# Two or four plain feed-forward blocks ahead of the paired ones

## The chip, the cores and the metric

The kernel runs on one core of a Trainium2 chip. The metric is the device time of one execution in microseconds; a kernel is run several times and the median is given. A single execution is also profiled, and the profile's span and rows belong to that execution alone.

The engines of the core that matter here are TensorE (PE in the profile; its weight loads are PEld), VectorE (DVE), ScalarE (ACT), GpSimd (POOL), which issues some transfers, and SyncE (SP), which issues most of the others. Each engine runs its own list of instructions in order and waits on semaphores for the others.

## The reference

One layer of a hybrid decoder, for 512 prompt positions and 64 sample positions (576 columns in all), with a model width of 1024:

```python
h = rms_norm(x, g_mix)
z = h @ w_in                      # pooling input, q, f, i, gate, ga, gb
ya = pool_branch(z) @ w_pool_up
yb = hgrn2_branch(z) @ w_hgrn_up
merged = sigmoid(ga) * ya + sigmoid(gb) * yb
x = x + merged @ w_out

h2 = rms_norm(x, g_ffn)
x = x + (silu(h2 @ w_ffn_gate) * (h2 @ w_ffn_up)) @ w_ffn_down

h3 = rms_norm(x, g_ple)
x = x + sigmoid(h3 @ w_ple_gate) * (p @ w_ple_proj)
y = rms_norm(x, g_final)
```

The feed-forward width is 2816, that is 22 blocks of 128 columns. All is float32.

## The kernel before

**Layout.** Activations lie transposed: a tile has 128 rows (features) and T = 576 columns (positions), so the width of 1024 is eight tiles. The columns are cut in two halves of HT = 288 (H0, H1). Every product is made with operands split in two: a high part in the rounded matmul format (fp32r) and a low part, which is what is missing; a product is high x high, high x low and low x high, three matmuls.

**A plain unit** (`mm`, L141 on) multiplies one 128-column block of weights by all eight tiles: 8 x 2 halves x 3 = 48 matmuls of 288 columns. A feed-forward block is a gate unit and an up unit, 96 matmuls. The weights of a plain unit need no work on VectorE: ScalarE makes the high part and the negated raw weights, and a transfer from POOL that adds (L88) completes the low part.

**A pair** (`pair`, L969) handles two neighbouring blocks at once by a Strassen-Winograd scheme: seven products in place of eight, each of 12 matmuls, 84 in all. Its products are named after the operand on the activation side: B11, S1, S2, B21, U3, and, done one pair later, U4 and B22. The order on TensorE is written out: `in_order` (with `state["pe"]`) hangs each group of matmuls behind the one before it. For a pair VectorE makes sums of the weights (`p_s1` L841 on, `p_s2` L846 on) and the low parts of two weight operands (`p_lo`, L855: B and C); ScalarE makes the high parts (L853), and two transfers from POOL complete the low parts of A and D.

**The forms.** The activation side of a pair, too, is made of sums: `form(k)` (L807) makes, from the residual tiles k and k+4, the normed values (two instructions at L811), four differences and sums of half width (L814 to L818), and splits them into the tiles fa, fb, fs and fu, each with a high part by ScalarE (L804) and a low part by VectorE (L805). There are four forms, k = 0 to 3, and every product of a pair runs over all four. They need `rn`, the reciprocal root of the mean square. The temporary tiles of a form are the same two rotating buffers (`ctile`, tags chi and clo) that later hold weight operand C.

**The order of the feed-forward stage.** NPL = 4 blocks, 0 to 3, go as plain units on residual tiles that carry the gain but not yet `rn`; `rn` is applied when a result leaves PSUM (L1122 and L1125), so these blocks can start before `rn` is known. It becomes known inside block 0. The forms are made beside the plain blocks: form 0 in block 0, forms 1 and 2 in block 1, form 3 in block 2, none in block 3. Beside the last plain block the first pair's weights are prepared (`p_all`, a generator stepped three times by `next(first)`). Then come the pairs: gate and up for blocks 4 and 5, 6 and 7, and so on to 20 and 21, with the down projections between them as soon as six activated blocks are there. The activated products of a gate and an up pair are turned into forms for the down projection by `ac_form`, for blocks 0 and 1 in the first pair and for 2 and 3 in the second.

Instructions of one engine are ordered by a scheduler that goes by program order and takes a later instruction when an earlier one is not ready in its own reckoning; so evictions and forms interleave on VectorE.

The same `pair` and `form` serve the gates of the mixer earlier, with four units of another projection beside the four forms.

Of the kernel before, what the change touches and what calls it, by code (L numbers as in the profile page):

```python
# [18 lines left out]
HT = 288  # L19
TA = 320  # L20
KD = 8
NPL = 4
EPS = 1e-6
WINDOWS = (2, 4, 8, 16)
UW = 15 + TP + 8 * 23
# [3 lines left out]
def trunk(ctx: ExitStack, tc: tile.TileContext, a, o):  # L29
# [43 lines left out]
    def hi_lo(pl=wp, tag="", bufs=3):  # L73
        return [pl.tile([P, 1024], F32R, name="w" + n, tag="w" + n + tag, bufs=bufs) for n in ("hi", "lo")]
# [34 lines left out]
    plain0 = len(seq)  # L109
    for m in range(NPL):  # L110
        seq += [a["w_ffn_gate"][m], a["w_ffn_up"][m]]
# [5 lines left out]
    def ahead(n_raw, n_split):  # L117
        while state["raw"] < min(n_raw, state["lim"]):
            i = state["raw"]
            raws[i] = raw_load(seq[i], seq[i].shape[-1])  # L120
            state["raw"] += 1
        while state["split"] < min(n_split, state["lim"]):
            i = state["split"]

            kw = dict(pl=es_pool["fp"], tag="z", bufs=2) if i >= len(seq) - 2 else {}
            if plain0 <= i < dn0 or i in (dn0 + 1, dn0 + 2) or up0 + 4 <= i < out0 and i % 2:
                kw["src"] = seq[i]
            splits[i] = split(raws.pop(i), seq[i].shape[-1], **kw)
            state["split"] += 1
# [643 lines left out]
    pairs = [(kind, m, 0) for m in range(0, KD, 2) for kind in ("ga", "gb")]  # L773
    for j in range(NPL, 22, 2):
        pairs.append(("gate", j, 0))
# [12 lines left out]
    def bank(t):  # L788
        return ps1.tile([P, 512], F32, name="b" + t, tag=t)[:, 0:HT]
# [3 lines left out]
    def two_banks():  # L793
        banks.reverse()
        return [bank(t) for t in banks[0]]

    def ctile(t, n=1024, dt=F32R):
        return fp.tile([P, 1024], dt, name="c" + t, tag="c" + t, bufs=2)[:, 0:n]
# [27 lines left out]
    def p_load(n):  # L826
        q = pr[n]
        q["ra"] = raw_load(q["src"][0], 2 * q["W"])
        q["rb"] = rb = fp.tile([P, 1024], F32, name="rb", tag="rb", bufs=2)
        nc.sync.dma_start(out=rb[:, 0:2 * q["W"]], in_=q["src"][1])  # L830

    def p_a(n):
        q = pr[n]
        q["A"] = u = hi_lo()
        split_dma(q["ra"], u, q["src"][0])

    def p_d(q):
        q["D"] = [fp.tile([P, 512], F32R, name="d" + x, tag="d" + x, bufs=2) for x in "hl"]
        split_dma(q["rb"][:, q["K"][1]], q["D"], q["src"][1][:, q["K"][1]])

    def p_s1(q):  # L841
        ra, rb, (K0, K1) = q["ra"], q["rb"], q["K"]
        tt(out=rb[:, K1], in0=rb[:, K0], in1=rb[:, K1], op=ADD)  # L843
        tt(out=rb[:, K0], in0=rb[:, K0], in1=ra[:, K0], op=SUB)

    def p_s2(q):  # L846
        ra, rb, (K0, K1) = q["ra"], q["rb"], q["K"]
        tt(out=ra[:, K0], in0=ra[:, K0], in1=rb[:, K1], op=SUB)  # L848
        tt(out=ra[:, K1], in0=ra[:, K1], in1=ra[:, K0], op=ADD)  # L849

    def p_hi(q, n, tiles, raw):
        q[n] = tiles
        nc.scalar.copy(out=tiles[0][:, 0:2 * q["W"]], in_=q[raw][:, 0:2 * q["W"]])  # L853

    def p_lo(q, n, raw):  # L855
        hi, lo = (t[:, 0:2 * q["W"]] for t in q[n])
        tt(out=lo, in0=q[raw][:, 0:2 * q["W"]], in1=hi.bitcast(F32), op=SUB)  # L857

    def p_b(q):
        p_hi(q, "B", hi_lo(), "rb")  # L860
        p_lo(q, "B", "rb")

    def prod(out, q, u, second, name, seeded):

        hi, lo = q[u]
        kw = {"skip_group_check": True} if seeded else {}
        n = q["W"] // P
        with in_order():
            for k in range(n):
                wh, wl = (w[:, second * q["W"] + k * P:second * q["W"] + (k + 1) * P] for w in (hi, lo))  # L870
                xh, xl = q["f"][name][k]
                nc.tensor.matmul(out=out, lhsT=wh, rhs=xh, start=k == 0 and not seeded, stop=False, **kw)  # L872
                nc.tensor.matmul(out=out, lhsT=wh, rhs=xl, start=False, stop=False, **kw)  # L873
                i = nc.tensor.matmul(out=out, lhsT=wl, rhs=xh, start=False, stop=k == n - 1, **kw)  # L874
        state["pe"] = i.ins

    def c22(q):
        q["cz"] = fp.tile([P, T], F32, name="cz", tag="cz", bufs=1)
        tt(out=q["cz"][:, H1], in0=q["b"], in1=q["p5"], op=ADD)  # L879

    def c21(q):
        tt(out=q["cz"][:, H0], in0=q["c"], in1=q["p5"], op=ADD)  # L882

    def p5_copy(q):
        q["p5"] = fp.tile([P, HT], F32, name="p5", tag="p5", bufs=1)
        nc.scalar.copy(out=q["p5"], in_=q["d"])
# [34 lines left out]
    def ac_split(j):  # L921
        t = gg.pop(j)
        xh, xl = (pl.tile([P, T], F32R, name="a" + tag, tag=tag) for pl, tag in ahl[2 * (j - 18):2 * (j - 17)])
        ac.append((xh, xl))
        nc.scalar.copy(out=xh, in_=t)
        tt(out=xl, in0=t, in1=xh.bitcast(F32), op=SUB)
# [42 lines left out]
    def pair(n):  # L969

        q, p = pr[n], pr[n - 1] if n > run[0] else None
        nq = pr[n + 1] if n + 1 < run[1] else None
        more = n + 2 < run[1]
        if more:
            p_load(n + 2)
        q.update({t: bank(t) for t in "ab"})
        prod(q["a"], q, "A", 0, "B11", False)
        if p:
            c22(p)
        if "B" not in q:  # L980
            p_b(q)
        seed = act(q["b"], q["a"], AF.Copy)
        if n == 0:
            with tc.issue_after(seed.ins):
                p_hi(nq, "A", hi_lo(), "ra")
            p_lo(nq, "A", "ra")
        q.update({t: bank(t) for t in "cd"})
        if p:
            prod(p["c"], p, "D", 0, "U4", True)
            c21(p)  # L990
            prod(p["b"], p, "C", 1, "B22", True)
        else:
            prod(q["d"], q, "B", 0, "S1", False)
        if nq:
            with tc.issue_after(seed.ins):
                p_d(nq)
            p_s1(nq)
        else:
            state["lim"] = len(seq) if run[0] else dn0
            ahead(state["use"] + 2, state["use"] + 1)  # L1000
        if p:
            evict(n - 1)
        if nq:
            p_s2(nq)
        prod(q["b"], q, "C", 0, "S2", True)
        x = act(q["c"], q["b"], AF.Copy)  # L1006
        with tc.issue_after(x.ins):
            if nq:
                p_hi(nq, "C", [ctile(t) for t in ("hi", "lo")], "ra")
        prod(q["a"], q, "A", 1, "B21", True)  # L1010
        if nq:
            p_lo(nq, "C", "ra")
        if more:
            with tc.issue_after(x.ins):
                p_a(n + 2)
        else:
            ahead(state["use"] + 3, state["use"] + 2)
        if p:
            prod(q["d"], q, "B", 0, "S1", False)
        p5_copy(q)  # L1020
        if n < run[0] + 2:
            if run[0]:
                ac_form(2 * (n - run[0]))
        elif pairs[n - 1][0] == "up" and pairs[n - 1][1] < 18:
            ac_form(pairs[n - 1][1])
        elif pairs[n - 1][0] == "up":
            for j in (18, 19):
                ac_split(j)
        prod(q["b"], q, "B", 1, "U3", True)
# [32 lines left out]
    run = [0, 8]  # L1062
# [11 lines left out]
    for n in range(*run):  # L1074
        pair(n)
# [25 lines left out]
    run[:] = run[1], len(pairs)  # L1101
    for j in range(NPL):
        if j == 0:
            spare = two_banks()
            pg, u = two_banks(), next_unit()
            mm(pg, u, hx, ks=range(0, 7))
            rn = rms(spare, [ctile(t, T) for t in ("hi", "lo")])
            mm(pg, u, hx, ks=range(7, KD))
        else:
            pg = unit_mm(hx, two_banks())  # L1110
        if j == NPL - 1:
            first = p_all(run[0])
            next(first)
            next(first)
        pu = unit_mm(hx, two_banks())
        for k in ((0,), (1, 2), (3,), ())[j]:
            form(k, g_ffn, rn, forms)
        if j == NPL - 1:
            next(first)
        g0, tg = tmpa(), tmpb()  # L1120
        for sl, z in zip((H0, H1), pg):
            tt(out=g0[:, sl], in0=z, in1=rn[:, sl], op=MULT)  # L1122
        act(g0, g0, AF.Silu)
        for sl, z in zip((H0, H1), pu):
            tt(out=tg[:, sl], in0=z, in1=rn[:, sl], op=MULT)  # L1125
        gg[j] = pers.tile([P, T], F32, name="stash", tag=("hh3", "hl7", "ssum")[j]) if j < NPL - 1 else g0
        tt(out=gg[j], in0=g0, in1=tg, op=MULT)
# [244 lines left out]
```

## Time and profile before

| what | us |
|---|---|
| median of 3 runs | 836.67 |
| lowest, highest | 836.52, 840.22 |
| the profiled execution's own time | 838.23 |
| its span in the profile | 836.2 |
| block 0 and its rms, from the first matmul to block 1 | 378.88 to 392.22 |
| block 1 | 392.22 to 404.94 |
| blocks 2 and 3 | 404.94 to 430.49 |
| first pair's first matmul | 430.49 |

The span is what the profile shows of the execution; the execution's own time is a little longer. Rows of a timeline give the start from the beginning of the span, the duration, the engine, the line of the kernel, the operation and its output and inputs; in square brackets stands the idle time of the engine ahead of it and what ended it. Tiles in PSUM are named ba, bb, bc and bd. Instructions of one engine overlap a little, so the distance from start to start is what one costs when the engine is full.

### The profile page before, as it was taken

What the parts mean: (1) busy time and instruction counts of PE and PEld (TensorE: products, weight loads), DVE (VectorE), ACT (ScalarE), POOL (GpSimd) and SP (SyncE); (2) the same over time, 40 slices, a digit from 0 to 9 for tenths busy, and PEclk for the clock granted to TensorE, in tenths of its full rate; (3) what the DMA queues carried; (4) which work ended last, traced back from release to release, by engine and by line L of the source; (5) the groups of instructions that cost most, each with busy time, mean ns of one, the idle gap of its engine ahead of it and who ended that gap; (6) DMA issues with size and microseconds to landing.
All of it is one profiled execution on the core that took longest, in us unless ns stands there. A gap on an engine that the chain in (4) does not pass through costs nothing.

```text
span 836.2 us, 15184 instructions
## 1 busy us (share of the span) xinstructions
PE 822.1 (98%) x6092; PEld 807.7 (97%) x6092; DVE 605.6 (72%) x1005; ACT 504.5 (60%) x826; POOL 114.1 (14%) x194
## 2 busy tenths in 40 slices
PE   8999999999999999999999999999999999999996
PEld 6999899999999999999999999999999999998996
DVE  7877776764787776547988688777787777558846
ACT  7356435666777665446667667766676666645534
POOL 6304110000111110000111121112211121000000
PEclk9999999999999999999999999999999999999998
DMA  7521220322747674246866787657777678453103
GB/s 233 164 84 51 76 105 29 126 105 80 181 107 183 165 172 140 76 108 144 186 130 142 149 208 194 157 123 175 181 173 164 132 158 214 113 156 101 52 1 113
DMA packets 38758, 111.95 MB, mean 134 GB/s; under 512 B 4896, under 2 KB 8992, under 8 KB 38688
## 3 DMA queue, kind: packets, MB, share of 16 engines
q1 hardware_dynamic: 24000, 74.51, 27.1%
q0 software_dynamic: 12528, 33.30, 23.5%
q10 hardware_dynamic: 2160, 3.19, 1.0%
q8 instruction: 47, 0.77, 0.4%
q14 instruction: 23, 0.19, 0.1%
HBM read 105.98 MB, written 5.00 MB: 133 GB/s over the span
## 4 chain that ended last, share of the span: by engine, by line
PE 91%; DVE 3%; DMA 2%; ACT 1%; issue 1%; POOL 1%; SPq 0%; DVEq 0%
PE bb L872 7%; PE bb L873 7%; PE bb L874 7%; PE mm L155 5%; PE mm L153 5%; PE mm L157 5%; PE ba L874 4%; PE ba L873 4%; PE ba L872 4%; PE bd L874 2%; PE bd L873 2%; PE bd L872 2%; PE bc L873 2%; PE bc L874 2%; PE bc L872 2%; PE ba L153 2%
## 5 line engine op out<-in xcount | busy, mean ns | idle before, releaser
L78 ACT CAST whi<-raw 128x1024 fp32r<-128x1024 f32 (+2 forms) x48 | 46.6, 972 | 70.6 <-PE mm L155 32.8
L153 PE MATMUL mm<-hh,whi 128*128 128x288 f32 x320 | 71.2, 304 | 1.1 <-DVE ta L358 0.9
L155 PE MATMUL mm<-hl,whi 128*128 128x288 f32 x320 | 70.8, 301 | 1.3 <-DVE hl L242 1.3
L157 PE MATMUL mm<-hh,wlo 128*128 128x288 f32 x320 | 69.5, 299 | 0.4 <-DVE wlo L79 0.4
L87 ACT ACTIVATE wlo<-raw 128x1024 fp32r<-128x1024 f32 (+1 forms) x49 | 49.2, 1004 | 26.3 <-PE ba L874 18.4
L79 DVE TENSOR_TENSOR wlo<-raw,whi 128x1024 fp32r<-128x1024 f32 (+2 forms) x48 | 56.7, 1184 | 10.4 <-ACT whi L78 9.8
L857 DVE TENSOR_TENSOR clo<-raw,chi 128x1024 fp32r<-128x1024 f32 (+1 forms) x38 | 43.3, 1140 | 27.8 <-ACT chi L853 27.7
L153 PEld LDWEIGHTS mm<-hh,whi 128*128 128x128 f32 x320 | 52.9, 193 | 4.0 <-ACT whi L78 1.6
L155 PEld LDWEIGHTS mm<-hl,whi 128*128 128x128 f32 x320 | 52.3, 191 | 2.5 <-DVE hl L242 1.9
L157 PEld LDWEIGHTS mm<-hh,wlo 128*128 128x128 f32 x320 | 52.3, 191 | 0.7 <-DVE wlo L79 0.6
L857 DVE TENSOR_TENSOR wlo<-rb,whi 128x1024 fp32r<-128x1024 f32 (+1 forms) x38 | 43.3, 1139 | 10.9 <-ACT whi L853 10.7
L853 ACT CAST chi<-raw 128x1024 fp32r<-128x1024 f32 (+1 forms) x38 | 36.9, 971 | 9.8 <-DVE raw L849 9.8
L853 ACT CAST whi<-rb 128x1024 fp32r<-128x1024 f32 (+1 forms) x38 | 37.3, 982 | 6.3 <-PE bb L873 2.8
L87 ACT ACTIVATE dl<-rb 128x512 fp32r<-128x512 f32 (+1 forms) x38 | 22.7, 598 | 30.0 <-PE bc L874 28.2
L1006 ACT ACTIVATE bc<-bb 128x288 f32<-128x288 f32 x38 | 15.0, 395 | 41.6 <-PE bb L874 41.6
L91 ACT CAST whi<-raw 128x1024 fp32r<-128x1024 f32 (+1 forms) x37 | 36.0, 972 | 0.0
L843 DVE TENSOR_TENSOR rb<-rb 128x512 f32<-128x512 f32 (+1 forms) x38 | 24.6, 647 | 8.0 <-ACT dh L91 8.0
L882 DVE TENSOR_TENSOR cz<-bc,p 128x288 f32<-128x288 f32 x38 | 17.3, 456 | 14.6 <-PE bc L874 14.3
L879 DVE TENSOR_TENSOR cz<-bb,p 128x288 f32<-128x288 f32 x38 | 17.3, 456 | 14.2 <-PE bb L874 9.1
L848 DVE TENSOR_TENSOR raw<-raw,rb 128x512 f32<-128x512 f32 (+1 forms) x38 | 24.6, 647 | 1.2 <-ACT whi L91 0.5
L88 POOL DMA_DIRECT2D wlo<-in_w_ffn_gate x13 | 11.1, 855 | 103.8 <-ACT wlo L87 103.8
L849 DVE TENSOR_TENSOR raw<-raw 128x512 f32<-128x512 f32 (+1 forms) x38 | 24.6, 647 | 0.8
(789 smaller groups left out, 3227.6 us busy)
## 6 DMA issues: line engine op xcount, KB each, us to landing
raw<-in_w_in SPq DMA_DIRECT2D x26, 512.0 KB, 3.4
raw<-in_w_ffn_gate SPq DMA_DIRECT2D x13, 512.0 KB, 4.1
raw<-in_w_ffn_up SPq DMA_DIRECT2D x13, 512.0 KB, 5.3
wlo<-in_w_ffn_gate POOLq DMA_DIRECT2D x13, 512.0 KB, 5.5
wlo<-in_w_ffn_up POOLq DMA_DIRECT2D x13, 512.0 KB, 6.3
rb<-in_w_ffn_gate SPq DMA_DIRECT2D x9, 512.0 KB, 4.6
rb<-in_w_ffn_up SPq DMA_DIRECT2D x9, 512.0 KB, 5.3
raw<-in_w_dn SPq DMA_DIRECT2D x12, 384.0 KB, 3.7
```

The costliest lines, as they stand in the source:

```text
L78: nc.scalar.copy(out=hi[:, cs], in_=raw[:, cs])
L79: tt(out=lo[:, cs], in0=raw[:, cs], in1=hi[:, cs].bitcast(F32), op=SUB)
L87: neg = act(lo, raw, AF.Copy, scale=-1.0)
L91: nc.scalar.copy(out=hi, in_=raw)
L153: nc.tensor.matmul(out=out[h], lhsT=wh, rhs=xh[:, h * HT:(h + 1) * HT], start=first, stop=False)
L155: nc.tensor.matmul(out=out[h], lhsT=wh, rhs=xl[:, h * HT:(h + 1) * HT], start=False, stop=False)
L157: i = nc.tensor.matmul(out=out[h], lhsT=wl, rhs=xh[:, h * HT:(h + 1) * HT], start=False, stop=last)
L853: nc.scalar.copy(out=tiles[0][:, 0:2 * q["W"]], in_=q[raw][:, 0:2 * q["W"]])
L857: tt(out=lo, in0=q[raw][:, 0:2 * q["W"]], in1=hi.bitcast(F32), op=SUB)
L872: nc.tensor.matmul(out=out, lhsT=wh, rhs=xh, start=k == 0 and not seeded, stop=False, **kw)
L873: nc.tensor.matmul(out=out, lhsT=wh, rhs=xl, start=False, stop=False, **kw)
L874: i = nc.tensor.matmul(out=out, lhsT=wl, rhs=xh, start=False, stop=k == n - 1, **kw)
```

## The change

The constant goes from 4 to 2. Two places that spelled out the old count go with it: the pairs in which `ac_form` takes plain blocks, and the distribution of the forms, which are now form 0 in block 0 and forms 1, 2 and 3 in block 1. Blocks 2 and 3 become a gate and an up pair, ahead of those for 4 and 5.

```diff
-NPL = 4
+NPL = 2
...
         p5_copy(q)
-        if n < run[0] + 2:
+        if run[0] <= n < run[0] + NPL // 2:
             if run[0]:
                 ac_form(2 * (n - run[0]))
         elif pairs[n - 1][0] == "up" and pairs[n - 1][1] < 18:
...
         pu = unit_mm(hx, two_banks())
-        for k in ((0,), (1, 2), (3,), ())[j]:
+        for k in ((0,), (1, 2, 3))[j]:
             form(k, g_ffn, rn, forms)
         if j == NPL - 1:
             next(first)
```

The list of pairs and the list of plain weights are built from NPL, so the two blocks leave the one and enter the other. `p_all` for the first pair is stepped beside block 1, the last plain one. The branch of `pair` on the mixer's side (run[0] = 0) does nothing in either kernel.

## The prediction

> **What bounds the kernel now.** The first view is the page: the share of each engine and the chain of waits.
>
> ```profile
> span 836.2 us, 15184 instructions
> PE 822.1 (98%) x6092; PEld 807.7 (97%) x6092; DVE 605.6 (72%) x1005; ACT 504.5 (60%) x826; POOL 114.1 (14%) x194
> PE 91%; DVE 3%; DMA 2%; ACT 1%; issue 1%; POOL 1%; SPq 0%; DVEq 0%
> ```
>
> TensorE (PE) is busy 98% of the span and carries 91% of the chain that ended last. So fewer matmuls shorten the kernel, and every wait put on TensorE lengthens it by its whole length. The averages hide that the change sits in one stage, so the second view is busy time by stretch, cut at the feed-forward blocks. The columns are the stretch, its length, the busy time (and instructions) of PE, PEld, DVE, ACT and POOL, the granted TensorE clock, the DMA share and GB/s.
>
> ```profile
> 389.21:415.44 26.23, 26.23 (x199) 26.16 (x199) 26.23 (x54) 19.88 (x29) 4.27 (x5) 1.00 0.78 167
> 404.94:417.76 12.82, 12.82 (x98) 12.75 (x97) 11.18 (x22) 8.23 (x12) 1.70 (x2) 1.00 0.87 188
> 417.76:430.49 12.73, 12.73 (x99) 12.73 (x98) 10.04 (x18) 7.27 (x10) 0.84 (x1) 1.00 0.65 155
> 438.45:449.57 11.12, 11.12 (x86) 11.12 (x85) 9.31 (x14) 9.48 (x17) 2.35 (x3) 1.00 0.60 144
> 449.57:460.70 11.13, 11.13 (x87) 11.13 (x86) 8.70 (x16) 6.77 (x13) 1.90 (x3) 1.00 0.57 126
> ```
>
> The second and third rows are plain blocks 2 and 3 (each a gate and an up unit, 96 matmuls); the last two are whole pairs (84 matmuls). TensorE has no idle time in any of them. The first row is the one to remember: from 389.21 to 415.44 VectorE (DVE) is busy 26.23 of 26.23 us. In this stretch TensorE and VectorE are both full, and only the order of the work keeps VectorE off the path. The third view, VectorE's instructions in order of time, says with what it is full.
>
> ```profile
> 385.53 3.77 DVE L277 RECIPROCAL rn<-rn 128x288 f32<-128x288 f32 x2 [1.03 <-ACT rn L276]
> 389.21 0.40 DVE L1122 TENSOR_TENSOR ta<-ba,rn 128x288 f32<-128x288 f32 x1
> 389.53 0.81 DVE L811 SCALAR_TENSOR_TENSOR chi<-res,C,rn 128x576 f32<-128x576 f32 x1
> ...
> 407.57 0.46 DVE L1122 TENSOR_TENSOR ta<-bb,rn 128x288 f32<-128x288 f32 x1
> 407.94 0.45 DVE L1125 TENSOR_TENSOR tb<-bc,rn 128x288 f32<-128x288 f32 x1
> 408.30 0.45 DVE L1125 TENSOR_TENSOR tb<-bd,rn 128x288 f32<-128x288 f32 x1
> ...
> 409.39 0.76 DVE L1127 TENSOR_TENSOR stash<-ta,tb 128x576 f32<-128x576 f32 x1
> 410.06 0.82 DVE L811 SCALAR_TENSOR_TENSOR clo<-res,C,rn 128x576 f32<-128x576 f32 x1
> ...
> 413.30 0.46 DVE L1122 TENSOR_TENSOR ta<-ba,rn 128x288 f32<-128x288 f32 x1
> 413.67 0.45 DVE L1122 TENSOR_TENSOR ta<-bb,rn 128x288 f32<-128x288 f32 x1
> 414.09 0.76 DVE L805 TENSOR_TENSOR fs3l<-chi,fs3h 128x576 fp32r<-128x576 f32 x1
> 414.77 0.75 DVE L805 TENSOR_TENSOR fu3l<-clo,fu3h 128x576 fp32r<-128x576 f32 x1
> 415.44 0.68 DVE L844 TENSOR_TENSOR rb<-rb,raw 128x512 f32<-128x512 f32 x1
> ```
>
> The reciprocal of the norm ends near 389.3, and nothing of the forms can start before it. The last form tile (fu3l) ends where the next instruction starts, at 415.44. In between stand the four forms, the evictions of blocks 0 and 1, and two instructions of block 2. An eviction is four instructions with 0.37 us from start to start (407.57, 407.94, 408.30) and one with 0.67 (409.39 to 410.06): 2.1 us. Block 2's two take 0.8 (413.30 to 414.09). So four forms take 26.2 - 2 x 2.1 - 0.8 = 21.2 us, **5.3 us each**. In the kernel before, the first pair reads them at 430.49, 15 us after they are done.
>
> ```profile
> 430.49 0.30 PE L872 MATMUL ba<-fa0h,whi 128*128 128x288 f32 x1
> ```
>
> **The change part by part.** *Removed and added on TensorE.* Blocks 2 and 3 go (404.94 to 430.49, 25.55 us) and two pairs come (11.12 + 11.13 = 22.25 us): **-3.3 us**. That is 192 matmuls for 168, at 0.133 us each. The new pairs load no more than the units they replace, and the pair rows above (DVE 9.31 and 8.70 of 11.1 us) leave each some 2 us of VectorE to spare.
>
> *Moved: the forms.* The first pair now starts where block 2 started, at 404.94. Its five products run in a fixed order, B11, S1, S2, B21, U3, each 12 matmuls (1.59 us). Without waits S1 would start at 406.5 and S2 at 408.1. B11 needs the last tile fa3; S1 needs fs3 and the low part of weight B; S2 needs the low part of weight C; the others need fb3 and fu3. All of it is VectorE work that can start at 389.2:
>
> - eviction of block 0, 2.1 us, and four forms, 21.2 us: 412.5;
> - the weight sums of the first pair and two subtractions for the low parts of B and C, priced by these rows (starts are some 0.08 us closer than durations): 3 x 0.6 + 2 x 1.15 = 4.1 us: 416.6;
> - the eviction of block 1, 2.1 us, as far as it comes ahead of these: up to 418.7.
>
> ```profile
> 420.00 0.69 DVE L848 TENSOR_TENSOR raw<-raw,rb 128x512 f32<-128x512 f32 x1 [0.48 <-ACT whi L91]
> 420.73 0.69 DVE L849 TENSOR_TENSOR raw<-raw 128x512 f32<-128x512 f32 x1
> 422.59 1.23 DVE L857 TENSOR_TENSOR clo<-raw,chi 128x1024 fp32r<-128x1024 f32 x1 [1.17 <-ACT chi L853]
> 425.14 1.22 DVE L857 TENSOR_TENSOR wlo<-rb,whi 128x1024 fp32r<-128x1024 f32 x1
> ```
>
> The low part of C cannot be made early: its tiles (chi, clo) are those in which the forms are made. The low part of B can; before, it came after C because its buffer was freed by the last plain block's gate unit (first row below), now it is freed by block 1's, which ends where its up unit starts (second row).
>
> ```profile
> 424.06 1.05 ACT L853 CAST whi<-rb 128x1024 fp32r<-128x1024 f32 x1 [1.50 <-PE bb L155]
> ...
> 398.58 0.29 PE L153 MATMUL bc<-hh,whi 128*128 128x288 f32 x1
> ```
>
> So I take B first: S1 starts near 416.5 and S2 near 417.7, the middle of 416.6 and 418.7. S2's first matmul with a low part stands 0.27 us behind its start, so the wait is 417.7 - 408.4 = 9.3 us; with casts on ScalarE between the links I take **+10 us** (bounds 6.9 and 12.0, worked out below). The matmuls behind the wait are all queued behind it: TensorE runs in order.
>
> *The other queues.* The raw weights of the first pair come where plain block 2's came, into the slot that block 1's gate unit frees; that load was issued at 380.84, and block 2's low part by POOL at 397.64, seven us ahead of 404.94. So no transfer becomes late.
>
> ```profile
> 380.84 0.33 SPq L70 DMA_DIRECT2D raw<-in_w_ffn_gate  x1
> 397.64 0.85 POOL L88 DMA_DIRECT2D wlo<-in_w_ffn_gate  x1 [7.17 <-ACT wlo L87]
> ```
>
> The vector work that is late (block 1's eviction, ac_form(0)) falls behind S2, where the pairs' spare 2 us each take it up; I cost it at nothing, and at up to 2 us if the second pair's sums come behind it.
>
> *The clock.* A wait of this length is something the trace before has only at its end.
>
> ```profile
> 760.00:766.00 6.00, 4.27 (x31) 4.19 (x32) 5.52 (x10) 3.62 (x5) 0.00 (x0) 1.00 0.18 74
> ...
> 828.00:831.00 3.00, 1.04 (x6) 0.72 (x6) 1.90 (x4) 2.53 (x6) 0.00 (x0) 0.81 0.00 0
> 831.00:833.00 2.00, 0.00 (x0) 0.00 (x0) 0.06 (x1) 0.00 (x0) 0.00 (x0) 0.50 0.92 349
> ```
>
> With 1.7 us idle of six the clock stays 1.00; when the matmuls end for good it falls to 0.50 (a mean of 0.81 over three us is 1.1 us at half) within some two us. How long it stays low after work resumes no row shows: nothing at one end, two whole products at half clock (24 matmuls x 0.133 = +3.2 us) at the other. The end row is the nearer one (idle after dense work), so I take one product: **+1.6 us**. The Trainium skill, TensorE: Matmul & The Clock Gate, section on the HAM clock gate, says that an idle window of about 3.4 us halves the clock and that a busy window of the same length restores it. By its figures one such gap would cost an estimated 1.7 us, and the sum would be +8.4 in place of +8.3; the end rows agree with the fall, and no run here shows the return.
>
> **Sum:** -3.3 + 10 + 1.6 = +8.3 us. The span of 836.2 would be 844.5, the profiled execution's own 838.23 us would be 846.5. The median of the runs, 836.67, stands 1.56 below that execution; the difference carries over: **845.0 us**.
>
> **The rivals.** *No loss of clock.* The wait comes in two pieces (B11's last three matmuls run between), and the gate does not close: -3.3 + 10 = +6.7, 843.4 us. For it: the 1.00 beside gaps of 1.7 us; against: each piece is over 3 us.
>
> *The best order.* VectorE leaves block 1's eviction and fu3 (0.67 us) until after the low part of C. S2 then starts at 416.6 - 0.67 - 0.6 (one weight sum done in the idle time ahead of the reciprocal) = 415.3, a wait of 6.9; without loss of clock the sum is +3.6, 840.3 us, within 0.5%.
>
> *Not slower at all.* The pair eats its forms in the order in which they are made, so the wait could vanish: -3.3, 833.4 us. It decides at the price of a form: all that S2 needs must be done by 408.4, so four forms have 408.4 - 389.2 - 2.1 - 4.1 = 13.0 us, 3.2 each. The rows say 5.3 with VectorE already full, so this is nearly excluded.
>
> *Longer.* The low part of C comes ahead of that of B, as before, and with block 1's eviction ahead of both: S1 waits from 406.8 to 418.7, 12.0 us, and the clock costs 3.2: +11.9, 848.6 us. With 2 us lost in the second pair, 850.6.
>
> **How the numbers follow.** Forecast 0.50; no loss of clock 0.20; best order 0.10; not slower 0.03; longer 0.17. A measurement here can tell about 0.5%, 4.2 us, from no change. Slower by more: 0.50 + 0.20 + 0.17 = 0.87; within: 0.10; faster: 0.03 (and -3.3 alone would hardly be told from no change). The range leaves out the 0.03, a part of the best order and the far end of the longest: 840.0 to 850.5.
>
> **What would show it.** In the changed kernel's profile: pairs follow block 1 and the forms' subtractions run to 412 or later, VectorE without idle time from 389 on. TensorE's first idle time should stand ahead of the matmul with fa3, released by VectorE or ScalarE; the next ahead of S1 or S2 (bd, bb), released by wlo or clo. Two more pairs of 11.1 us should be found later, without new gaps. The granted clock of the stretch behind the wait shows 0.5 or 1.00. I am wrong if TensorE waits under 6.9 us there, if a DMA releases it, or if gaps appear in the later pairs.

## The result, and the profile after

| | median us | lowest to highest | runs |
|---|---|---|---|
| before | 837.25 | 836.43 to 840.22 | 9 |
| changed | 845.83 | 841.40 to 846.91 | 9 |

The changed kernel is slower: ratio 1.008, with a 95% interval from 1.0062 to 1.0098. The forecast was 845.0 us. The profiled execution of the changed kernel took 841.75 us (before: 838.23).

The page of the changed kernel shows the place: first the busy shares, then TensorE's busy tenths and its granted clock in 40 slices of 21 us, then the chain of waits.

```profile
span 840.0 us, 15155 instructions
PE 819.1 (98%) x6068; PEld 804.6 (96%) x6068; DVE 613.4 (73%) x1014; ACT 509.2 (61%) x837; POOL 113.8 (14%) x194
...
PE   8999999999999999999599999999999999999996
...
PEclk9999999999999999999799999999999999999998
...
PE 86%; DVE 6%; DMA 2%; issue 2%; ACT 2%; POOL 1%; SPq 0%; DVEq 0%
```

TensorE has 24 matmuls and 3.0 us of work less, as the change intends, and still the span is 3.8 us longer. Of 40 slices one differs from the page before: the twentieth (399 to 420 us), where TensorE's busy tenths fall to 5 and its clock to 7. VectorE's share of the chain doubles, from 3% to 6%. TensorE's waits between 380 and 431 us say who held it (us in total, times, longest):

```profile
PE bd L874 <- DVE wlo L857: 3.8, 1, 3.8
PE ba L872 <- ACT fa3h L804: 2.7, 1, 2.7
PE ba L873 <- DVE fa3l L805: 1.6, 1, 1.6
PE ba L873 <- DVE fa2l L805: 0.3, 1, 0.3
```

All four stand in the first pair. TensorE's instructions there, in order of time:

```profile
403.33 0.29 PE L872 MATMUL ba<-fa0h,whi 128*128 128x288 f32 x1
...
404.96 0.29 PE L874 MATMUL ba<-fa2h,wlo 128*128 128x288 f32 x1
407.98 0.40 PE L872 MATMUL ba<-fa3h,whi 128*128 128x288 f32 x1 [2.73 <-ACT fa3h L804]
410.02 0.61 PE L873 MATMUL ba<-fa3l,whi 128*128 128x288 f32 x1 [1.64 <-DVE fa3l L805]
...
415.11 0.61 PE L874 MATMUL bd<-fs0h,wlo 128*128 128x288 f32 x1 [3.76 <-DVE wlo L857]
...
417.67 0.44 PE L872 MATMUL bb<-fs0h,chi 128*128 128x288 f32 x1
```

The pair starts at 403.33, runs out of forms at 405.25, waits for the fourth form in two pieces, and then for the low part of weight B. S1 gets that at 415.11 and S2 (bb) starts at 417.67. The waits sum to 0.30 + 2.73 + 1.64 + 3.76 = 8.4 us. VectorE's instructions say what it was doing meanwhile:

```profile
385.04 0.69 DVE L844 TENSOR_TENSOR rb<-rb,raw 128x512 f32<-128x512 f32 x1 [2.14 <-DMA raw<-in_w_ffn_gate]
385.65 3.76 DVE L277 RECIPROCAL rn<-rn 128x288 f32<-128x288 f32 x2
389.33 0.40 DVE L1122 TENSOR_TENSOR ta<-ba,rn 128x288 f32<-128x288 f32 x1
...
409.52 0.45 DVE L805 TENSOR_TENSOR fa3l<-chi,fa3h 128x288 fp32r<-128x288 f32 x1
...
413.84 1.21 DVE L857 TENSOR_TENSOR wlo<-rb,whi 128x1024 fp32r<-128x1024 f32 x1
414.98 0.44 DVE L1122 TENSOR_TENSOR ta<-ba,rn 128x288 f32<-128x288 f32 x1
...
416.07 1.21 DVE L857 TENSOR_TENSOR clo<-raw,chi 128x1024 fp32r<-128x1024 f32 x1
```

The rows left out here follow in the same way: from 385.65 one instruction starts before the one ahead of it has ended, until the low part of B (wlo) ends at 415.05 and beyond. The ScalarE instruction named by the 2.7 us wait (fa3h) is a cast of what VectorE has just made, so it is VectorE again. New against before is the first row: a sum of weights (L844) waits 2.14 us for a transfer, and the reciprocal stands behind it.

Then busy time by stretch of the changed kernel (stretch, length, busy PE, PEld, DVE, ACT, POOL with counts, clock, DMA share, GB/s): the first three pairs, and two pieces of the first.

```profile
403.33:422.95 19.62, 11.20 (x62) 10.16 (x61) 19.55 (x37) 11.16 (x18) 1.70 (x2) 0.74 0.37 94
422.95:434.09 11.14, 11.14 (x87) 11.14 (x85) 8.98 (x14) 9.34 (x15) 1.70 (x2) 1.00 0.68 166
434.09:445.22 11.13, 11.13 (x87) 11.13 (x85) 9.57 (x17) 8.13 (x14) 2.56 (x3) 1.00 0.77 169
405.25:407.98 2.73, 0.00 (x1) 0.00 (x0) 2.73 (x5) 1.59 (x3) 0.00 (x0) 1.00 0.00 0
408.52:418.76 10.24, 4.98 (x19) 4.63 (x20) 10.24 (x19) 7.21 (x11) 1.70 (x2) 0.50 0.43 75
```

In the first row TensorE is busy 11.20 of 19.62 us and VectorE 19.55. The last row is the whole stretch in which the granted clock is 0.50. The same pair took 7.96 us in the kernel before, whose row is:

```profile
430.49:438.45 7.96, 7.96 (x62) 7.96 (x61) 6.51 (x13) 6.02 (x10) 1.75 (x3) 1.00 0.58 100
```

So the loss in the first pair is 19.62 - 7.96 = 11.7 us: 8.4 of waits and 3.2 of matmuls that ran at half clock or, as the first behind a wait, took longer (0.40 us in place of 0.29 at 407.98). With the 3.3 us that two pairs save against two plain blocks, the change costs 11.7 - 3.3 = +8.4 us there; the forecast sum was +8.3. (The two spans differ by only 3.8 us: this execution of the kernel before lost time elsewhere, which the last section looks at.)

### The profile page after: what moved, and what is told of

The parts are those of the page before. It is cut to its first block, busy times and chain, and to the rows that moved or that the text cites. A ratio compares the mean times of both kernels' runs of the same rounds, so it can differ in the third digit from the quotient of the medians.

```text
span 840.0 us, 15155 instructions
## 1 busy us (share of the span) xinstructions
PE 819.1 (98%) x6068; PEld 804.6 (96%) x6068; DVE 613.4 (73%) x1014; ACT 509.2 (61%) x837; POOL 113.8 (14%) x194
## 4 chain that ended last, share of the span: by engine, by line
PE 86%; DVE 6%; DMA 2%; issue 2%; ACT 2%; POOL 1%; SPq 0%; DVEq 0%
PE bb L872 7%; PE bb L873 7%; PE bb L874 7%; PE mm L155 5%; PE mm L153 5%; PE mm L157 5%; PE ba L874 5%; PE ba L873 5%; PE ba L872 5%; PE bd L874 2%; PE bd L872 2%; PE bd L873 2%; PE bc L873 2%; PE bc L874 2%; PE bc L872 2%
## 5 line engine op out<-in xcount | busy, mean ns | idle before, releaser
L857 DVE TENSOR_TENSOR clo<-raw,chi 128x1024 fp32r<-128x1024 f32 (+1 forms) x40 | 45.7, 1143 | 27.0 <-ACT chi L853 26.9
L87 ACT ACTIVATE wlo<-raw 128x1024 fp32r<-128x1024 f32 (+1 forms) x47 | 47.1, 1002 | 23.9 <-PE ba L874 20.4
L857 DVE TENSOR_TENSOR wlo<-rb,whi 128x1024 fp32r<-128x1024 f32 (+1 forms) x40 | 45.7, 1143 | 12.3 <-ACT whi L853 12.3
L853 ACT CAST chi<-raw 128x1024 fp32r<-128x1024 f32 (+1 forms) x40 | 39.0, 975 | 9.4 <-DVE raw L849 9.3
L853 ACT CAST whi<-rb 128x1024 fp32r<-128x1024 f32 (+1 forms) x40 | 39.4, 986 | 5.7 <-PE bb L873 3.2
L91 ACT CAST whi<-raw 128x1024 fp32r<-128x1024 f32 (+1 forms) x39 | 38.0, 975 | 0.0
L844 DVE TENSOR_TENSOR rb<-rb,raw 128x512 f32<-128x512 f32 (+1 forms) x40 | 25.8, 645 | 2.5 <-DMA raw<-in_w_ffn_gate 2.1
```

Of the source, the lines that this page charges most:

```text
L87: neg = act(lo, raw, AF.Copy, scale=-1.0)
L91: nc.scalar.copy(out=hi, in_=raw)
```

## The experiments

Theory: the work that VectorE must do between the norm's reciprocal and S2 is longer than block 1 covers, and this backlog sets the wait; slow matmuls come on top where VectorE's work does not hide them. Rivals: the weights' chain (sums, casts, low parts) sets the wait and not the forms; the bunching of three forms beside block 1 does harm by itself; the clock loss costs nothing of its own, since VectorE sets the pace; the late reciprocal is the cause. One number compares the profiles: the **head**, from the first product of the first pair to the first product of the third. It is 7.96 + 11.12 = 19.08 us in the kernel before and 30.76 in the changed one. Ratios are against the kernel before on the same chip.

**The changed kernel again**, on the chip of the next three.

> The changed kernel once more, to be the base of the others. Its first profile had 8.4 us of TensorE waits at the head of the first pair and a granted clock of 0.50 for 9 us there. Backlog theory: the waits are set by VectorE's queue and are 8.4 us again within 0.3. Clock theory for the scatter of the runs (841.4 to 846.9): a profile of an execution near 845 shows a longer stretch of granted clock at 0.5, there or elsewhere, and no other wait; rival: it shows a longer wait.

Median 844.04, ratio 1.0081 (1.0060 to 1.0102). Head 30.58; the waits stand at the same instructions with 2.72, 1.64 and 3.75 us. The result repeats. The profile, of an execution of 844.54 us, shows the same 10.24 us at half clock in the first pair and one more such stretch, of 3.41 us, at 767.61; the last section comes back to it. The first pair:

```profile
403.66:423.12 19.46, 11.35 (x63) 10.55 (x61) 19.13 (x36) 11.48 (x19) 1.71 (x2) 0.74 0.38 94
```

**One form only.** Forms 1 to 3 are left out of the feed-forward stage and form 0 stands in for them; the result is not the layer's any more, only the time is of interest.

```diff
     def form(k, g, rn, forms):
+        if g is g_ffn and k:
+            for n in FORMS:
+                forms[n].append(forms[n][-1])
+            return
```

> The changed kernel with form 0 alone: the products of the feed-forward pairs use its tiles for all four k, so the vector and scalar work of forms 1 to 3 (3 x 5.3 us of VectorE) is left out. Backlog theory: the head of the first pair has no wait over 0.5 us, the clock stays 1.00, and only the matmul saving is left: 3.3 us faster than the kernel before (ratio 0.996). Rival (the first pair's weights are late, their sums, low parts or transfers): a wait for wlo of some 3.8 us stays and the ratio is 1.000 or more.

Median 834.33, ratio 0.9959 (0.9942 to 0.9976): 3.4 us faster than before by the ratio. TensorE has no wait in the two pairs, by the stretches of this kernel:

```profile
405.03:413.00 7.97, 7.97 (x62) 7.97 (x61) 5.89 (x11) 6.02 (x10) 1.75 (x3) 1.00 0.85 185
413.00:424.12 11.12, 11.12 (x86) 11.12 (x85) 9.30 (x14) 9.47 (x16) 2.27 (x3) 1.00 0.68 167
```

The weights alone keep nobody waiting, so that rival falls. And with the forms gone the change brings what the matmuls are worth, 3.4 us (2.0 to 4.9) for a forecast of 3.3.

**Forms early, four plain blocks.** The kernel before with the changed distribution of the forms.

```diff
-        for k in ((0,), (1, 2), (3,), ())[j]:
+        for k in ((0,), (1, 2, 3), (), ())[j]:
```

> The kernel before (four plain blocks) with its forms placed as in the changed kernel: form 0 in block 0, forms 1 to 3 in block 1, none in blocks 2 and 3. Backlog theory: the place of the forms costs nothing as long as blocks 2 and 3 cover them; no TensorE wait from 378 to 440 us, ratio 1.000 within 0.002. Rival (bunched forms slow the plain blocks by themselves, through the ScalarE queue or PSUM that is freed late): waits inside blocks 1 to 3 and a ratio of 1.003 or more.

Median 836.42, ratio 0.9995 (0.9976 to 1.0013). From inside block 0 to the end of block 3 TensorE is busy 46.14 of 46.17 us:

```profile
386.00:432.17 46.17, 46.14 (x348) 45.86 (x348) 40.76 (x74) 31.41 (x44) 5.12 (x6) 1.00 0.70 158
```

Making three forms in a row costs nothing that shows; needing them at once does.

**The weight sum behind the reciprocal.** L844 of the first pair is queued behind the reciprocals, so that its wait for the transfer holds nothing else.

```diff
-                nc.vector.reciprocal(out=rn[:, hs], in_=rn[:, hs])
+                state["rec"] = nc.vector.reciprocal(out=rn[:, hs], in_=rn[:, hs]).ins
...
-        tt(out=rb[:, K0], in0=rb[:, K0], in1=ra[:, K0], op=SUB)
+        with tc.issue_after(state["rec"]) if q is pr[8] else nullcontext():
+            tt(out=rb[:, K0], in0=rb[:, K0], in1=ra[:, K0], op=SUB)
```

> The changed kernel with one VectorE instruction moved: the first pair's second weight sum (L844) is queued behind the reciprocals of the norm. In the changed kernel it stood ahead of them and waited 2.1 us for the raw weights, and the reciprocal started 1.7 us later than its input was there. Backlog theory: every form is 1.7 us earlier, less the 0.6 that the sum then costs behind them or among them; the waits fall from 8.4 to some 7 us, and the time by 1 to 2 us against the changed kernel. Rival (VectorE's start does not matter, since something else sets fa3, fs3 or wlo): waits of 8.4 us and no change.

Median 844.74, ratio 1.0086 (1.0063 to 1.0109), no better. The expected 1 to 2 us did not come. The reciprocal now starts when its input is there, but the sum (L845 here, one line further down) stands among the forms:

```profile
384.96 3.77 DVE L277 RECIPROCAL rn<-rn 128x288 f32<-128x288 f32 x2 [1.03 <-ACT rn L276]
...
395.35 0.68 DVE L845 TENSOR_TENSOR rb<-rb,raw 128x512 f32<-128x512 f32 x1
```

The first pair as a whole:

```profile
404.36:423.78 19.42, 11.51 (x62) 10.71 (x61) 18.73 (x34) 11.46 (x18) 1.75 (x3) 0.74 0.38 95
```

From the pair's first product to its first matmul with the low part of B it is 10.79 us in place of the 11.19 of the changed kernel run again: 0.4 us gained. The whole pair takes 19.42 us in place of 19.46, since the stretch at half clock is again 10.24 us long (410.33 to 420.57) and ends later in the pair. Ahead of the reciprocal the sum had been done in time that was partly idle; behind it, it costs its own length in the full queue. So the late reciprocal is a small part of the loss. How late the transfer is differs from execution to execution: VectorE waits 2.14 us for it in the first profile of the changed kernel, 1.58 in the second.

**Fillers in the waits.** Matmuls into a bank that is overwritten before it is read (20 and 10 ahead of B11's last two waits, 26 ahead of S1) keep TensorE working where it would wait.

```diff
+    def filler(q, count):
+        for _ in range(count):
+            with in_order():
+                i = nc.tensor.matmul(out=q["c"], lhsT=q["A"][0][:, 0:P], rhs=q["f"]["B11"][0][0], start=True, stop=True)
+            state["pe"] = i.ins
...
+                if k == 3 and j < 2:
+                    filler(q, (20, 10)[j])
...
+        filler(q, 26)
```

> The changed kernel with 56 more matmuls in TensorE's idle time at the head of the first pair (20 ahead of B11's last three, 10 behind the first of those, 26 ahead of S1; at 0.133 us each 7.4 us). They read tiles that are ready and write to PSUM that is seeded later, so nothing waits for them. Clock theory: the granted clock stays 1.00, the 24 matmuls of S1 and S2 cost 3.2 us less, and the time falls by about 3 us against the changed kernel on the same chip (844.0 to some 841, ratio to the kernel before 1.004). Rival (the clock costs nothing, the waits are all): no change, 844. Rival (the filler takes the place of work): slower than 844.

Median 844.91, ratio 1.0097 (1.0071 to 1.0122): nothing gained, where 3 us had been expected. The clock stays at 1.00 in both pairs:

```profile
404.60:422.46 17.86, 16.35 (x118) 15.55 (x117) 17.86 (x33) 10.54 (x18) 1.70 (x2) 1.00 0.42 102
422.46:434.78 12.32, 11.40 (x86) 11.16 (x85) 8.93 (x15) 9.44 (x14) 2.56 (x3) 1.00 0.61 150
```

But the first pair is only 1.6 us shorter than in the changed kernel run again, on another chip (19.46), with VectorE busy 17.86 of 17.86, and the second pair is 1.2 longer. The waits of this kernel say why:

```profile
PE bb L872 <- ACT bb L1006: 0.9, 1, 0.9
PE bd L874 <- DVE wlo L857: 0.8, 1, 0.8
PE bb L874 <- DVE clo L857: 0.4, 1, 0.4
```

TensorE at full speed reaches S1 and S2 early and waits there for the same low parts. So about half of the 3.2 us of slow matmuls had been hidden behind VectorE's work, and 1.6 us were the clock's own price in the first pair. And TensorE now reaches the second pair before ScalarE has copied the result (bb) that S2 starts from. ScalarE's instructions in that pair:

```profile
424.06 1.06 ACT L87 ACTIVATE wlo<-raw 128x1024 fp32r<-128x1024 f32 x1 [2.59 <-DMA raw<-in_w_ffn_gate]
...
426.91 1.04 ACT L853 CAST whi<-rb 128x1024 fp32r<-128x1024 f32 x1
427.86 0.39 ACT L1006 ACTIVATE bb<-ba 128x288 f32<-128x288 f32 x1
```

The copy takes 0.39 us, but stands behind four weight steps of 1 us (the first and the last are shown), and these behind a transfer of raw weights. The queue of SyncE issued that transfer at 417.81:

```profile
417.81 0.33 SPq L70 DMA_DIRECT2D raw<-in_w_ffn_gate  x1
```

and VectorE, in this kernel's timeline, had read the raw tile for the low part of C until 416.56 + 1.22 = 417.78. The queue's own waits name that instruction:

```profile
SPq L70 <- DVE clo L857: 1.8, 1, 1.8
```

So the backlog reaches the second pair by a detour: low part, buffer, transfer, ScalarE.

**Three forms.** Form 3 alone is left out, as above with `k == 3`.

> The changed kernel with forms 0 to 2 only: the fourth step of each product uses form 2's tiles, so 5.3 us of VectorE work of form 3 is left out. Backlog theory: every later instruction of VectorE moves up by 5.3, so the waits fall from 8.1 to about 2.8 us in all and the clock loss to 0 to 1.6; 7 us faster than the changed kernel (about 837, ratio 0.999 within 0.003). Rival (the low part of B, or its weights, is late by itself): the wait for wlo stays near 3.8 us and the gain is under 4.

Median 839.22, ratio 1.0024 (1.0006 to 1.0043). The head is 12.61 + 11.73 = 24.34 us, so the loss against 19.08 falls from 11.5 (the changed kernel again) to 5.3, by 6.2 us for a form priced at 5.3. TensorE waits 2.7 us for the low part of B in the first pair, where 2.8 us were expected in all, and 0.3 for ScalarE's copy in the second. The median is less far down than expected: the ratio falls by 0.0057, some 4.8 us, for a forecast of 7, and stays above that of the kernel before. The first pair:

```profile
404.71:417.32 12.61, 9.87 (x63) 9.48 (x62) 11.87 (x20) 7.99 (x13) 1.70 (x2) 0.86 0.59 138
```

**No reciprocal.** The feed-forward norm's two reciprocals (3.8 us of VectorE) are left out.

```diff
-                nc.vector.reciprocal(out=rn[:, hs], in_=rn[:, hs])
+                if keep:
+                    nc.vector.reciprocal(out=rn[:, hs], in_=rn[:, hs])
```

> The changed kernel without the two reciprocals of the feed-forward norm (rn is left as the root), so VectorE's forms can start 3.7 us earlier. Backlog theory: the start of VectorE's queue moves all of it, the waits fall by 3.7 to some 4.4 us, the clock loss by 0 to 1.6; 4 to 5 us faster than the changed kernel (839 to 840, ratio 1.002 to 1.004). Rival (ScalarE's casts, or TensorE's own order, set fa3, fs3 and wlo): less than 2 us faster.

Median 840.45, ratio 1.0034 (1.0016 to 1.0052), as expected. The head is 26.40, 4.2 us shorter than that of the changed kernel run again (30.58):

```profile
403.93:419.21 15.28, 10.54 (x63) 10.08 (x62) 14.96 (x28) 9.27 (x15) 1.70 (x2) 0.78 0.49 120
```

This run takes work from VectorE alone, where the runs without forms also spare ScalarE their casts, so it is VectorE that sets the pace. In the run with three forms and in this one, 5.3 and 3.8 us of vector work taken from the queue ahead of S2 shorten the head by 6.2 and 4.2 us, a little more than their length, whatever that work computes.

**Both mends.** The weight sum behind the reciprocal, and 20, 8 and 20 fillers; the whole computation is done.

> The changed kernel with the weight sum behind the reciprocals and 48 filler matmuls: the computation is complete. Backlog and clock theory together: waits and filler of 7.7 us in all, clock 1.00, about 3.5 us faster than the changed kernel (840.5, ratio 1.003), so still no faster than the kernel before, since some 7.7 us of vector work stay ahead of S1 and S2 for 3.3 us of matmuls saved.

Median 844.62, ratio 1.0090 (1.0060 to 1.0119). The head is 29.71, only 0.9 us under 30.58, and the median is 4 us above the forecast. The first pair takes 17.65 us, 1.8 us less than with the weight sum moved but no fillers (19.42); the second again waits 0.7 us for ScalarE's copy.

**And ScalarE's order.** As the last, with the four weight steps of the third pair queued behind the second pair's copy.

```diff
+        if run[0] and n == run[0] + 1:
+            with tc.issue_after(seed.ins):
+                p_a(n + 1)
...
-        elif more:
+        if fill:
+            pass
+        elif more:
```

> The kernel with the weight sum moved and the filler, and the third pair's first weight work on ScalarE (the negated raw of operand A, which waits for a raw transfer) put behind the second pair's seed copy. In the kernel with filler alone that instruction waited 2.6 us for its transfer and stood ahead of the second pair's cast of C and its seed, and TensorE waited 0.9 us for the seed in the second pair (12.3 us in place of 11.1). Queue theory: the second pair is 11.1 us again and the head 0.9 us shorter; the median is some 1 us lower, which the runs can hardly tell. Rival (VectorE's low part of C is late by itself): the wait stays, released by clo. Other rival: the third pair's operand A now comes late, and the third pair waits for wlo.

Median 843.0 (against 836.85 on its chip), ratio 1.0083 (1.0052 to 1.0113). The second pair has no wait any more, and the head is 28.77:

```profile
404.95:422.59 17.64, 15.16 (x111) 14.46 (x109) 17.64 (x32) 11.44 (x19) 1.70 (x2) 1.00 0.43 104
422.59:433.72 11.13, 11.13 (x86) 11.13 (x85) 9.89 (x16) 9.59 (x15) 2.56 (x3) 1.00 0.77 167
```

That the copy stood behind the weight steps is shown. The first pair keeps its 17.64 us with VectorE busy in all of them: with the clock at 1.00 throughout, a loss of 9.7 us against a saving of 3.3. The 1.8 us by which the head shrank are too few to be seen in this ratio, whose interval is some 5 us wide. No version with two plain blocks and the whole computation beats the kernel before. Useful products in the place of the fillers were not tried.

## Why the prediction was right, and where not

**What bounds the kernel, and the direction: right.** TensorE was full, the forms had 15 us of cover from blocks 2 and 3, and the change took it away. Without three of the forms the same change is 3.4 us faster; with them it is slower by the forecast amount. The rival "not slower at all" needed forms of 3.2 us each; leaving one out brought 6.2 us of head, clock included.

**The place: right.** The first wait of any length was forecast ahead of the matmul with fa3, the next ahead of S1 or S2 with wlo or clo. They are at fa3h, fa3l and wlo. S1 was forecast near 416.5 and S2 near 417.7; S1's first matmul with a low part ran at 415.11 and S2 at 417.67. The low part of B came ahead of that of C, as assumed, and three of the five instructions of block 1's eviction fell between them (from 414.98). That S2 came within 0.1 us of its forecast is luck: in this execution the pair started 1.6 us earlier than assumed (403.33 for 404.94), and the reciprocal 1.7 us later than its input was there, which the prediction did not foresee. Counted from the pair's first product, S2 was forecast 12.8 us on; it came 14.3 us on here, 13.8 when the kernel was run again, and 12.4 with the fillers.

**The matmuls, -3.3 us: right** (-3.4, with an interval from -4.9 to -2.0, in the run with one form).

**The wait, +10 us, and the clock, +1.6: right, the sum and the split.** The head lost 11.7 us for 11.6 forecast. The first profile alone seems to say that the parts were wrong, since it shows 8.4 us of waits and 3.2 of slow matmuls. But "+10" is the time by which VectorE's work holds up the pair, and a part of that time is filled with slow matmuls instead of waiting. What each costs, the fillers show: with the clock at 1.00 the first pair loses 17.86 - 7.96 = 9.9 us, and the clock adds 1.6 (19.46 against 17.86; with the weight sum moved 1.8, 19.42 against 17.65). Each of these is a difference of two executions on two chips, and the size of the clock term was a middle between nothing and 3.2, so that it fell so close is in part luck. The rival "no loss of clock" priced it in the same way, and in the first pair it would have been right. It does not show in the fillers' median, since the second pair gives 1.2 us back; with ScalarE's order mended as well, the head is 1.8 us shorter than that of the changed kernel run again, and the medians are too coarse to confirm it.

**"No transfer becomes late": wrong.** The raw weights for the sum at L844 arrive 2.14 us after VectorE is free for it (1.58 when run again), and since VectorE takes its instructions in order, the reciprocal stands behind them. The check in the prediction looked at when the transfer is issued and at the pair's start at 404.94, not at the first instruction that reads it nor at what is queued behind that. The best-order rival even counted one sum in the idle time ahead of the reciprocal as a gain. The net price is small: moving the sum away brought 0.4 us at S1 and nothing that shows in the head.

**"The late vector work costs nothing, up to 2 us in the second pair": right as it ran, for a reason not given.** The later pairs are clean (11.14, 11.13). But with fillers the second pair loses 0.7 to 0.9 us in a wait, through a buffer, a transfer and ScalarE's queue; without fillers the slow clock of the first pair brings TensorE there 1.6 us later, and ScalarE has the time. The term was put at nothing; with the clock held up it is worth 0.9 to 1.2 us.

**How long the clock stays low.** The prediction said that no row shows the return; now several do. TensorE went idle at 405.25, and the clock was 0.50 from 408.52 to 418.76: it fell 3.3 us after the idle time began, although one matmul ran at 407.98, and was back 3.7 us after work resumed at 415.11. The Trainium skill, TensorE: Matmul & The Clock Gate, section on the HAM clock gate, gives windows of about 3.4 us for both, and these two figures agree. Other runs show that the 3.3 us are no fixed delay. First the run with three forms (the gap, the work behind it, and the stretch at half clock), then the run without reciprocals:

```profile
406.73:409.47 2.74, 0.00 (x0) 0.00 (x0) 2.74 (x5) 2.74 (x5) 1.14 (x2) 1.00 0.03 3
409.47:410.50 1.03, 1.03 (x7) 1.03 (x8) 1.03 (x4) 1.03 (x2) 0.56 (x1) 1.00 0.95 151
410.50:413.91 3.41, 3.41 (x16) 3.26 (x15) 3.41 (x7) 1.26 (x3) 0.00 (x0) 0.50 0.86 171
...
408.69:415.51 6.82, 4.56 (x19) 4.56 (x20) 6.82 (x12) 4.73 (x7) 1.18 (x2) 0.50 0.83 157
```

In the first the gap is only 2.74 us long, and the clock falls 1.0 us after it is over. In the second it falls 2.0 us after TensorE went idle. What is common is the length at half clock: 3.41, 6.82 and 10.24 us, one, two and three times the same 3.41. These traces look as if the clock were decided anew every 3.41 us, wherever in that time a gap begins. So a gap of 2.7 us can cost a whole stretch, and a wait in two pieces (2.73 and 1.64 us here) does not keep the clock up.

## What to carry to other kernels

Before work is taken from the bound engine, ask what it covered on the in-order engines that feed it: here 3.3 us of matmuls were saved and 11.7 us of delay uncovered, on an engine that is busy 73% of the span and 100% of this stage. A clock loss that comes from a wait overlaps with what is waited for: count only the slow matmuls that the awaited engine does not hide (here 1.6 of 3.2 us), and ask what the engine, once it is fast, will wait for next. Follow a moved transfer to the first instruction that reads it, and to what stands behind that instruction in its queue.

## What the hardware showed that was not expected

Single executions of one kernel differ by more than most effects here (the kernel before: 832.86 to 840.61 us in 23 runs on one chip). One place can be seen in the profiles: from 100 to 140 us, a stage that the change doesn't touch. First the kernel before:

```profile
100.00:140.00 40.00, 40.00 (x288) 37.82 (x288) 25.85 (x51) 19.16 (x36) 4.99 (x14) 0.96 0.19 68
```

and the changed kernel:

```profile
100.00:140.00 40.00, 40.00 (x299) 37.89 (x298) 25.92 (x51) 19.17 (x36) 4.99 (x14) 1.00 0.19 68
```

TensorE is busy 40.00 us in both, but with a mean clock of 0.96 it gets 11 matmuls less done: 40 x 0.04 = 1.6 us. That is as much as block 2 before (404.94) starts later than the first pair after (403.33). No wait explains it. The loss stands in one place, behind 16 matmuls of only 8 columns each (first row; the second is the stretch at half clock):

```profile
135.01 1.95 PE L593 MATMUL aux<-lt,S 128*128 128x8 f32 x16
...
136.98:140.40 3.42, 3.42 (x15) 3.32 (x16) 2.87 (x8) 1.35 (x3) 0.00 (x0) 0.50 0.00 0
```

It is again a stretch of 3.41 us at half clock, which costs 1.7 us. Nine of the eleven profiles have one or two such stretches between 100 and 190 us, ten in all; each is 3.41 us long and begins within 0.6 us of the end of such a group of narrow matmuls. The group runs four times in the kernel before and is followed by a fall once; what decides remains open. This also goes a long way to explain the scatter. A stretch of 3.41 us lowers the mean granted clock of an execution by 1.7 in 836, or 0.002. Of the 23 executions above, the three fastest (832.86 to 834.42) have a mean clock of 0.998, and the eight with 0.992 took 837.82 to 840.12 us: three stretches more, an estimated 5.1 us, between groups whose middles lie 4.8 us apart.

Another place is the entry of the stage behind the feed-forward, where TensorE's waits behind 700 us are, in the kernel before,

```profile
PE bc L153 <- DVE res L1166: 2.6, 2, 1.8
```

and in the changed kernel

```profile
PE bc L153 <- DVE res L1166: 0.9, 1, 0.9
```

while the changed kernel run again shows 1.8 there. So of the 8.4 us that the change costs in these two pairs, 1.6 and 1.7 are covered up in the spans, and 1.3 more that I did not trace: 3.8 us remain, where the medians differ by 8.6. Two spans are not to be subtracted without looking for such places.
